# Decoder trunk, one core: cache loads moved to GpSimd's queue, and another order at the end of the first norm

## The chip, the cores and the metric

The kernel runs on one core of a Trainium2 chip. The metric is the device time of one execution in microseconds (us), the median over several runs. A profile is one execution under the hardware profiler. Its engines are PE (TensorE matmul), DVE (VectorE), ACT (ScalarE), POOL (GpSimd) and SP (SyncE, which issues most transfers).

## The reference, cut to what matters

One decoder layer runs on 1024 prompt tokens and on 8 decode samples that share the weights. All arithmetic is float32.

```python
z = x @ w_in                                   # all branches and gates in one projection
# branch C, decode: each sample attends to its own 256 memory tokens, 4 heads of width 256
s = jnp.einsum('bthd,bmhd->bhtm', q, mk).astype(jnp.float32) * (XHEAD_DIM ** -0.5)
p = jax.nn.softmax(s, axis=-1).astype(mv.dtype)
...
return jnp.einsum('bhtm,bmhd->bthd', p, mv).reshape(B, T, XW)
...
h = layer_norm(ALPHA * x + merged @ w_out, ln1_g, ln1_b)        # the first norm
gt, up = jnp.split(h @ w_gate_up, 2, axis=-1)
h = layer_norm(ALPHA * h + (jax.nn.silu(gt) * up) @ w_down, ln2_g, ln2_b)
```

## The kernel before, in words

The 1032 tokens (1024 + 8) lie along the free dimension, the channels along the 128 partitions. Every product is done as three matmuls: each operand is cut into a high part, rounded by ACT (`CAST ..h`, line 79), and a low part, subtracted by DVE (`TENSOR_TENSOR ..l`, line 80), and PE adds high x high, high x low and low x high. A weight's low part is needed for the third matmul of each group only. Most projections use one level of Strassen's scheme: seven products instead of eight, with sums of quarter tiles made by DVE.

**The projection** (about 60 to 690 us) is a list of 30 units of seven products; a product takes PE some 2.9 us, and weights are cut three products ahead. After each product `pump` advances side work by a step: the gated recurrence `lru` and the transposes of the value rows `v_rows` after each one, and `dec_mem`, the decode samples' memory attention, after every second one. `dec_mem` runs once per head (4 heads). Its inner `fetch` loads a 256 KB tile of the key cache (`dck`) or value cache (`dcv`) and, for every second sample, the broadcast row that it is multiplied with (`dckq`, `dcvq`); `dots` then multiplies and sums on DVE (line 840). Each tag has two buffers, so a load waits for the `dots` two samples back. All of these 92 loads are issued by SP, in one queue with the weight loads (`ur`) and the stores. `v_rows` transposes on PE into a PSUM tile of which there is one buffer (`vt`, tag "o"); ACT (line 385) and DVE (line 386) empty it before the next transpose may start.

**The first norm** works by quarters of the tokens. `quarter_norm` of the last quarter (q = 3) ends after the output projection; PE meanwhile runs `plain_gate_up`, the first two feed-forward units f = 0 and 1 done plainly, quarter by quarter: gate product `fg`, ACT's tanh and DVE's line 1170 (`ft`), up product `fu`, DVE's line 1173 (`G`). `ft` releases the PSUM buffer of `fg` (two for even quarters, two for odd ones), `G` that of `fu` (three in all). The norm takes the root on ACT (`n1rs`), the reciprocal on DVE (line 1075), multiplies both halves (`R30`, `R31`; line 1077), applies gain and shift on ACT (line 1082, four steps a half), stores, and cuts into `hh30`/`hl30` and `hh31`/`hl31`. `h_combos` then makes the quarter sums for Strassen (`ht`, `hth`, `htl`, sums written into `R..`). The weights of f = 1 are cut in halves: `wfg10`, `wfg11` for the gate, `wfu10`, `wfu11` for up.

The framework's scheduler sets each engine's order from its own model of time. Each engine then runs its list strictly in that order and waits by semaphores. `tc.issue_after(ins)` keeps what is written inside it behind `ins` in the list of the engine of `ins`.

Of the kernel before, what the change touches and what calls it, by code (L numbers as in the profile page):

```python
# [12 lines left out]
AF = mybir.ActivationFunctionType  # L13
ALU = mybir.AluOpType
# [4 lines left out]
P = 128  # L19
# [22 lines left out]
QN = T // 4  # L42
# [16 lines left out]
V_G1, V_B1, V_G2, V_B2, V_SNK, V_SNKD, V_EPS, V_N = 88, 96, 104, 112, 120, 136, 137, 138  # L59


class Builder:
# [754 lines left out]
    def dec_mem(self, h):  # L817

        nc, io, ph = self.nc, self.io, self.dp
        qr = self.dram.tile([NB, 256], F32, name=f"dcq{h}")  # L820
        self.dec_rows(self.qdc, 2 * h, qr, "c")
        sc = ph.tile([P, 2, NB], F32, tag="dsc", name=f"dcs{h}", bufs=1)
        rows = {}

        def fetch(kind, b, src, row=None):
            if row is not None and b % 2 == 0:
                rows[kind] = ph.tile([P, 512], F32, tag="dq", name=f"dc{kind}q{b}_{h}", bufs=2)
                nc.sync.dma_start(rows[kind].rearrange("p (b d) -> p b d", b=2), row[b:b + 2, :].partition_broadcast(P))
            t = ph.tile([P, 512], F32, tag="dk", name=f"dc{kind}{b}_{h}", bufs=2)
            nc.sync.dma_start(t.rearrange("p (t d) -> p t d", t=2), src)  # L830
            return t

        keys = lambda b: fetch("k", b, io["cmk"][b, :, h * 256:(h + 1) * 256].rearrange("(t p) d -> p t d", p=P), qr)
        vals = lambda b, row: fetch("v", b, io["cmvT"][b, h * 256:(h + 1) * 256, :].rearrange("(f p) k -> p f k", p=P),
                                    row)

        def dots(t, row, b, dst):
            for e in range(2):
                junk = ph.tile([P, 256], F32, tag="dj", name=f"dcj{b}_{h}_{e}", bufs=1)
                nc.vector.scalar_tensor_tensor(junk, t[:, e * 256:(e + 1) * 256], 1.0,  # L840
                                               row[:, (b % 2) * 256:(b % 2 + 1) * 256], op0=ALU.mult, op1=ALU.mult,
                                               accum_out=dst(e))

        nxt = keys(0)
        yield
        for b in range(NB):
            t, row = nxt, rows["k"]
            nxt = keys(b + 1) if b + 1 < NB else vals(0, None)
            dots(t, row, b, lambda e: sc[:, e, b:b + 1])
            yield  # L850
        ps = self.bank("o", f"dct{h}")
        for kt in range(2):
            nc.tensor.transpose(ps[:NB, kt * P:(kt + 1) * P], sc[:, kt, :], self.ident)
        pr = ph.tile([NB, 256], F32, tag="dp", name=f"dcp{h}", bufs=1)
        st = self.sm.tile([P, 8], F32, tag="cst", name=f"dcst{h}", bufs=4)
        nc.vector.tensor_reduce(st[:NB, 0:1], ps[:NB, :256], axis=AX.X, op=ALU.max, negate=True)
        nc.scalar.activation(pr, ps[:NB, :256], AF.Exp, bias=st[:NB, 0:1], scale=1.0, accum_out=st[:NB, 1:2])
        nc.vector.reciprocal(st[:NB, 2:3], st[:NB, 1:2])
        nc.vector.tensor_scalar_mul(pr, pr, st[:NB, 2:3])
        pd = self.dram.tile([NB, 256], F32, name=f"dcpd{h}")  # L860
        nc.sync.dma_start(pd, pr)
        rows["v"] = ph.tile([P, 512], F32, tag="dq", name=f"dcvq_{h}", bufs=2)
        nc.sync.dma_start(rows["v"].rearrange("p (b d) -> p b d", b=2), pd[0:2, :].partition_broadcast(P))
        yield
        for b in range(NB):
            t, row = nxt, rows["v"]
            nxt = vals(b + 1, pd) if b + 1 < NB else None
            dots(t, row, b, lambda e: self.cdec[:, 2 * h + e, b:b + 1])
            yield
# [187 lines left out]
    def quarter_norm(self, q, s1, h):  # L1057

        nc, r, vec = self.nc, self.R, self.vec
        cast = lambda a: a.unsqueeze(1).to_broadcast([P, 4, QN])  # L1060
        yield
        mu = self.col_mean(s1, QN, f"n1mu{q}")
        sq = []
        for kh in range(2):
            nc.vector.tensor_sub(r[q, kh], r[q, kh], cast(mu))
            sq.append(self.tq.tile([P, 4, QN], F32, tag=f"q{q}{kh}", name=f"sq{q}{kh}", bufs=2))
            nc.scalar.activation(sq[kh], r[q, kh], AF.Square)
        nc.vector.tensor_add(sq[0], sq[0], sq[1])
        nc.vector.tensor_add(sq[0][:, 0:2, :], sq[0][:, 0:2, :], sq[0][:, 2:4, :])
        nc.vector.tensor_add(sq[0][:, 0, :], sq[0][:, 0, :], sq[0][:, 1, :])  # L1070
        yield
        var = self.col_mean(sq[0][:, 0, :], QN, f"n1va{q}")
        rs = self.ph.tile([P, QN], F32, tag="rs", name=f"n1rs{q}", bufs=1)
        nc.scalar.activation(rs, var, AF.Sqrt, bias=vec[:, V_EPS:V_EPS + 1])
        nc.vector.reciprocal(rs, rs)
        for kh in range(2):
            nc.vector.tensor_mul(r[q, kh], r[q, kh], cast(rs))
            h[q, kh] = self.quarter_pair(q, kh, "h")
            for k in range(4):
                m = 4 * kh + k  # L1080
                v = r[q, kh][:, k, :]
                nc.scalar.activation(v, v, AF.Identity, bias=vec[:, V_B1 + m:V_B1 + m + 1],
                                     scale=vec[:, V_G1 + m:V_G1 + m + 1])
            nc.sync.dma_start(self.scr["h"][:, 4 * kh:4 * kh + 4, q * QN:(q + 1) * QN], r[q, kh])
            self.split(*h[q, kh], r[q, kh])
        self.norm_end = self.last_lo
# [70 lines left out]
    def plain_gate_up(self, f, h, steps):  # L1157

        nc, io = self.nc, self.io
        wg = self.weights(io["wgu"][f], D, f"wfg{f}")  # L1160
        wu = self.weights(io["wgu"][NF + f], D, f"wfu{f}")
        out = self.zt(f"G{f}")
        for q in range(4):
            x = [tuple(a[:, k % 4, :] for a in h[q, k // 4]) for k in range(KT)]
            pg = self.bank(("s", "t")[q % 2], f"fg{f}_{q}")[:, :QN]
            self.mm3(pg, list(zip(wg, x)))
            self.norm_step()
            t = self.ph.tile([P, QN], F32, tag="gt", name=f"ft{f}_{q}", bufs=3)
            nc.scalar.activation(t, pg, AF.Tanh, scale=0.5)
            nc.vector.scalar_tensor_tensor(t, t, 1.0, pg, op0=ALU.add, op1=ALU.mult)  # L1170
            pu = self.bank("mm", f"fu{f}_{q}")[:, :QN]
            self.mm3(pu, list(zip(wu, x)))
            nc.vector.tensor_mul(out[:, q * QN:(q + 1) * QN], t, pu)
            if f or q:
                with self.tc.issue_after(self.norm_end):
                    next(steps, None)
        nc.sync.dma_start(self.scr["f"][:, f, :], out)
# [281 lines left out]
class FinishDown:  # L1459


    scale = SHARE
# [158 lines left out]
```

## Time and profile before

| | |
|---|---|
| median of 3 runs | 1936.51 us (1936.05 to 1939.27) |
| profiled execution | 1938.83 us, of which the span 1937.1 us |
| granted PE clock | 0.995 of full speed |
| POOL transfers issued | 16 stores of memory keys and values, 16 accumulating stores near the end |
| bytes moved | 303.20 MB, 157 GB/s over the span |

A row of a group of instructions gives line, engine, operation, output<-input, count, then busy time in us and mean ns of one, then the idle time just before them and what ended it. A row of the timeline gives start, duration, engine, line, and in brackets the idle time before it with what it waited for. A row of the waits gives who waited for whom, the total in us, the number of times and the longest.

### The profile page before, as it was taken

To read this page: it belongs to the slowest core of one execution; us is meant where nothing else is said; L and a number is where in the kernel's file an instruction comes from. 1 tells how busy PE (TensorE), PEld (TensorE's weight loads), DVE (VectorE), ACT (ScalarE), POOL (GpSimd) and SP (SyncE) were. 2 spreads that over 40 slices of the span, in tenths; PEclk is the share of its full clock that TensorE was granted. 3 is DMA by queue.
4 is the path that set the end of the run, shared out by engine and by line. 5 is a ranking of instruction groups with operands and counts; after the bars stand their busy time and mean duration, and the time that the engine had idled before them with its cause. 6 is when DMAs were issued, how large, how long until landed. Compare 5 with 4: busy or idle time off the path is not lost.

```text
span 1937.1 us, 37999 instructions
## 1 busy us (share of the span) xinstructions
PE 1901.0 (98%) x14716; PEld 1869.5 (97%) x14716; DVE 1389.0 (72%) x2738; ACT 1001.8 (52%) x2115; POOL 117.0 (6%) x168
## 2 busy tenths in 40 slices
PE   9999999999999999999999999999999999999996
PEld 8999999999999998888899999999999999999996
DVE  7878887877866655378887557775667667858467
ACT  6555565555655644388775234543433434636424
POOL 1000001110000000022110000000000000001001
PEclk9999999999999999999999999999999999999998
DMA  8545555446423376667534351123245345768542
GB/s 308 179 146 173 168 182 167 140 150 210 169 83 137 117 240 222 196 173 208 152 98 152 110 197 58 60 99 99 93 154 195 96 134 182 254 161 233 137 143 88
DMA packets 171637, 303.20 MB, mean 157 GB/s; under 512 B 19568, under 2 KB 86208, under 8 KB 171456
## 3 DMA queue, kind: packets, MB, share of 16 engines
q1 hardware_dynamic: 168384, 290.22, 45.8%
q0 software_dynamic: 3072, 10.55, 2.7%
q8 instruction: 115, 1.88, 0.4%
q14 instruction: 66, 0.54, 0.1%
HBM read 214.79 MB, written 90.09 MB: 157 GB/s over the span
## 4 chain that ended last, share of the span: by engine, by line
PE 84%; ACT 5%; DMA 4%; DVE 4%; issue 1%; SPq 0%; ACTq 0%; DVEq 0%
PE ub L250 5%; PE ub L248 5%; PE ub L249 5%; PE ubfg L248 4%; PE ubfg L249 4%; PE ubfg L250 4%; PE ud L250 3%; PE ud L249 3%; PE ud L248 3%; PE udfg L248 2%; PE udfg L249 2%; PE udfg L250 2%; PE op L120 2%; PE op L122 2%; PE op L121 2%; PE brs L120 2%
## 5 line engine op out<-in xcount | busy, mean ns | idle before, releaser
L605 ACT ACTIVATE bp<-bp,bst 128x257 f32<-128x257 f32 (+1 forms) x128 | 62.8, 493 | 17.7 <-DVE bst L601 17.3
L248 PE MATMUL ub<-th,u_4h 128*128 128x258 f32 x240 | 67.8, 283 | 1.3 <-ACT u2s L274 1.3
L248 PE MATMUL ub<-th,u_0h 128*128 128x258 f32 x240 | 68.0, 284 | 0.7 <-ACT zb L1490 0.6
L250 PE MATMUL ub<-th,u_4l 128*128 128x258 f32 x240 | 68.2, 284 | 0.0
L250 PE MATMUL ub<-th,u_0l 128*128 128x258 f32 x240 | 68.2, 284 | 0.0
L250 PE MATMUL ub<-th,u_2l 128*128 128x258 f32 x240 | 68.2, 284 | 0.0
L250 PE MATMUL uc<-th,u_3l 128*128 128x258 f32 x240 | 68.2, 284 | 0.0
L250 PE MATMUL ud<-th,u_1l 128*128 128x258 f32 x240 | 68.1, 284 | 0.0
L250 PE MATMUL ud<-th,u_5l 128*128 128x258 f32 x240 | 68.1, 284 | 0.0
L250 PE MATMUL ub<-th,u_6l 128*128 128x258 f32 x240 | 68.1, 284 | 0.0
L248 PE MATMUL ub<-th,u_6h 128*128 128x258 f32 x240 | 67.9, 283 | 0.0
L248 PE MATMUL uc<-th,u_3h 128*128 128x258 f32 x240 | 67.9, 283 | 0.0
L248 PE MATMUL ub<-th,u_2h 128*128 128x258 f32 x240 | 67.8, 283 | 0.0
L248 PE MATMUL ud<-th,u_5h 128*128 128x258 f32 x240 | 67.8, 282 | 0.0
L248 PE MATMUL ud<-th,u_1h 128*128 128x258 f32 x240 | 67.7, 282 | 0.0
L249 PE MATMUL ub<-tl,u_6h 128*128 128x258 f32 x240 | 67.7, 282 | 0.0
L249 PE MATMUL ud<-tl,u_5h 128*128 128x258 f32 x240 | 67.7, 282 | 0.0
L249 PE MATMUL uc<-tl,u_3h 128*128 128x258 f32 x240 | 67.6, 282 | 0.0
L249 PE MATMUL ub<-tl,u_4h 128*128 128x258 f32 x240 | 67.6, 282 | 0.0
L249 PE MATMUL ud<-tl,u_1h 128*128 128x258 f32 x240 | 67.6, 282 | 0.0
L249 PE MATMUL ub<-tl,u_0h 128*128 128x258 f32 x240 | 67.6, 282 | 0.0
L249 PE MATMUL ub<-tl,u_2h 128*128 128x258 f32 x240 | 67.6, 282 | 0.0
(954 smaller groups left out, 8228.3 us busy)
## 6 DMA issues: line engine op xcount, KB each, us to landing
ur<-win SPq DMA_DIRECT2D x120, 256.0 KB, 2.9
urfg<-wgu SPq DMA_DIRECT2D x80, 256.0 KB, 2.6
scr_f<-G SPq DMA_DIRECT2D x22, 516.0 KB, 3.2
f<-scr_f SPq DMA_DIRECT2D x16, 516.0 KB, 5.7
fs<-scr_t SPq DMA_DIRECT2D x16, 516.0 KB, 8.3
dck<-cmk SPq DMA_DIRECT2D x32, 256.0 KB, 3.7
dcv<-cmvT SPq DMA_DIRECT2D x32, 256.0 KB, 2.8
st<-scr_q SPq DMA_DIRECT2D x32, 256.0 KB, 5.1
```

Of the source, the lines that this page charges most:

```text
L120: nc.tensor.matmul(ps, sh, mh, start=opens and i == 0, stop=False)
L121: nc.tensor.matmul(ps, sh, ml, start=False, stop=False)
L122: self.last_mm = nc.tensor.matmul(ps, sl, mh, start=False, stop=closes and i == last).ins
L248: mm(sh[:, w], xh, start=opens and k == 0, stop=False)
L249: mm(sh[:, w], xl, start=False, stop=False)
L250: self.last_mm = mm(sl[:, w], xh, start=False, stop=k == 3).ins
L605: nc.scalar.activation(x, x, AF.Exp, bias=st[:, g:g + 1], scale=-1.0, accum_out=st[:, 4 + g:5 + g])
```

## The change

`fetch` issues its loads of cache tiles and of row pairs from GpSimd's queue instead of SP's (64 + 28 transfers). The first row pair of the values (line 863 before) stays on SP. Two more `yield`s let `dec_mem` pause one step longer ahead of its first load and ahead of its first value `dots`. In `quarter_norm`, the third and fourth gain-and-shift step of each half of the last quarter go from ACT to DVE. In `plain_gate_up`, `G` of quarters 0 and 1 is kept behind the norm's last reciprocal, `G` of quarters 2 and 3 behind the last `hl`.

```diff
@@ fetch, in dec_mem
-                nc.sync.dma_start(rows[kind].rearrange("p (b d) -> p b d", b=2), row[b:b + 2, :].partition_broadcast(P))
+                nc.gpsimd.dma_start(rows[kind].rearrange("p (b d) -> p b d", b=2), row[b:b + 2, :].partition_broadcast(P))
             t = ph.tile([P, 512], F32, tag="dk", name=f"dc{kind}{b}_{h}", bufs=2)
-            nc.sync.dma_start(t.rearrange("p (t d) -> p t d", t=2), src)
+            nc.gpsimd.dma_start(t.rearrange("p (t d) -> p t d", t=2), src)
@@ dec_mem
+        yield
         nxt = keys(0)
         yield
...
         nc.sync.dma_start(rows["v"].rearrange("p (b d) -> p b d", b=2), pd[0:2, :].partition_broadcast(P))
+        yield
         yield
@@ quarter_norm
-        nc.vector.reciprocal(rs, rs)
+        self.norm_root = nc.vector.reciprocal(rs, rs).ins
...
-                nc.scalar.activation(v, v, AF.Identity, bias=vec[:, V_B1 + m:V_B1 + m + 1],
-                                     scale=vec[:, V_G1 + m:V_G1 + m + 1])
+                gain, shift = vec[:, V_G1 + m:V_G1 + m + 1], vec[:, V_B1 + m:V_B1 + m + 1]
+                if q == 3 and k > 1:
+                    nc.vector.tensor_scalar(v, v, gain, shift, op0=ALU.mult, op1=ALU.add)
+                else:
+                    nc.scalar.activation(v, v, AF.Identity, bias=shift, scale=gain)
@@ plain_gate_up
-            nc.vector.tensor_mul(out[:, q * QN:(q + 1) * QN], t, pu)
+            with self.tc.issue_after(self.norm_root if q < 2 else self.norm_end):
+                nc.vector.tensor_mul(out[:, q * QN:(q + 1) * QN], t, pu)
```

The lists of the engines move in two places of the program, the projection and the end of the first norm. The lines after the edits are numbered up to six higher, so `ft` is L1175 and `G` L1179 in the new kernel.

**First place: DVE at the end of the norm's last quarter.** In these names the two digits after `R`, `hh`, `hl` are quarter and half, and those after `ft` and `fu` are f and quarter. Before:

```order
L1173 TENSOR_TENSOR G0_16171<-ft0_1_16297,fu0_1_16300 128x258
L1075 RECIPROCAL n1rs3_16274<-n1rs3_16274 128x258
L1077 TENSOR_TENSOR R30_15877<-R30_15877,n1rs3_16274 128x1032
L1077 TENSOR_TENSOR R31_15879<-R31_15879,n1rs3_16274 128x1032
L1170 SCALAR_TENSOR_TENSOR ft0_2_16357<-ft0_2_16357,fg0_2_16332 128x258
L1173 TENSOR_TENSOR G0_16171<-ft0_2_16357,fu0_2_16360 128x258
L80 TENSOR_TENSOR hl30_16279<-R30_15877,hh30_16278 128x1032
```

The same place now:

```order
L1077 RECIPROCAL n1rs3_16274<-n1rs3_16274 128x258
L1179 TENSOR_TENSOR G0_16171<-ft0_1_16297,fu0_1_16300 128x258
L1079 TENSOR_TENSOR R30_15877<-R30_15877,n1rs3_16274 128x1032
L1079 TENSOR_TENSOR R31_15879<-R31_15879,n1rs3_16274 128x1032
L1086 TENSOR_SCALAR R30_15877<-R30_15877,vec_65 128x258 x2
L1086 TENSOR_SCALAR R31_15879<-R31_15879,vec_65 128x258 x2
L1175 SCALAR_TENSOR_TENSOR ft0_2_16357<-ft0_2_16357,fg0_2_16332 128x258
L80 TENSOR_TENSOR hl30_16279<-R30_15877,hh30_16278 128x1032
```

The reciprocal stands ahead of `G` of quarter 1, four gain-and-shift steps are added, and `G` of quarter 2 is gone from ahead of `hl30`.

**Second place: DVE just behind, where `h_combos` and the weights of f = 1 are made, and PE there.** `wfg10_l` is the low part of the first half of f = 1's gate weights. DVE before, from the last `hl` on:

```order
L80 TENSOR_TENSOR hl31_16289<-R31_15879,hh31_16288 128x1032
L1145 TENSOR_TENSOR ht1_0_16326<-R00_15043,R20_15611 128x1032
L80 TENSOR_TENSOR wfg10_l_16459<-wfg1r0__16456,wfg10_h_16458 128x512
L1148 TENSOR_TENSOR R20_15611<-R21_15613,R20_15611 128x1032
L80 TENSOR_TENSOR htl1_0_16329<-ht1_0_16326,hth1_0_16328 128x1032
L1149 TENSOR_TENSOR R00_15043<-R20_15611,R00_15043 128x1032
```

DVE now:

```order
L80 TENSOR_TENSOR hl31_16289<-R31_15879,hh31_16288 128x1032
L1150 TENSOR_TENSOR ht1_0_16326<-R00_15043,R20_15611 128x1032
L1179 TENSOR_TENSOR G0_16171<-ft0_2_16357,fu0_2_16360 128x258
L1153 TENSOR_TENSOR R20_15611<-R21_15613,R20_15611 128x1032
L80 TENSOR_TENSOR htl1_0_16329<-ht1_0_16326,hth1_0_16328 128x1032
L1154 TENSOR_TENSOR R00_15043<-R20_15611,R00_15043 128x1032
L1175 SCALAR_TENSOR_TENSOR ft0_3_16417<-ft0_3_16417,fg0_3_16392 128x258
L80 TENSOR_TENSOR htl4_0_16447<-R20_15611,hth4_0_16446 128x1032
L91 SCALAR_TENSOR_TENSOR htl2_0_16389<-R00_15043,hth2_0_16388 128x1032
L1179 TENSOR_TENSOR G0_16171<-ft0_3_16417,fu0_3_16420 128x258
L1158 TENSOR_TENSOR R00_15043<-R00_15043,R01_15045 128x1032
L80 TENSOR_TENSOR wfg10_l_16459<-wfg1r0__16456,wfg10_h_16458 128x512
```

`wfg10_l` went from second behind the last `hl` to eleventh. PE now, from the last matmul of f = 0 on (before, the last row here followed the first one at once):

```order
L122 MATMUL fu0_3_16420<-hh31_16288,wfu01_l_16168 128x258
L120 MATMUL fu1_0_16509<-hh00_15482,wfu10_h_16470 128x258
L121 MATMUL fu1_0_16509<-hl00_15483,wfu10_h_16470 128x258
L120 MATMUL fu1_1_16569<-hh10_15748,wfu10_h_16470 128x258
L121 MATMUL fu1_1_16569<-hl10_15749,wfu10_h_16470 128x258
L120 MATMUL fg1_3_16664<-hh30_16278,wfg10_h_16458 128x258
L121 MATMUL fg1_3_16664<-hl30_16279,wfg10_h_16458 128x258
L120 MATMUL fu1_2_16629<-hh20_16014,wfu10_h_16470 128x258
L121 MATMUL fu1_2_16629<-hl20_16015,wfu10_h_16470 128x258
L122 MATMUL fg1_0_16481<-hh00_15482,wfg10_l_16459 128x258
```

Eight matmuls that need no low part moved ahead of the first that does. The two on `fg1_3` reuse the PSUM buffer of `fg0_3`, those on `fu1_2` the one of `fu0_3`.

**Third place: DVE in the projection, beside the transposes of the value rows.** `v0` to `v7` are the value rows, `dcj` the output of `dots` (digits: sample, head, half), `u18_..`, `us19_..` the weight parts and sums of units 18 and 19. Before:

```order
L386 TENSOR_TENSOR v2_6237<-vt2_6234,v2_6237 128x4x64
L80 TENSOR_TENSOR u18_4l_6299<-us18_4_6296,u18_4h_6298 128x512
L232 TENSOR_TENSOR us19_2_6511<-us19_1_6475,ur19_00_6288 128x512
L386 TENSOR_TENSOR v3_6278<-vt3_6275,v3_6278 128x4x64
L840 SCALAR_TENSOR_TENSOR dcj5_3_0_6565,dcs3_6032<-dck5_3_6469,dckq4_3_6380 128x256
L840 SCALAR_TENSOR_TENSOR dcj5_3_1_6567,dcs3_6032<-dck5_3_6469,dckq4_3_6380 128x256
L80 TENSOR_TENSOR u18_5l_6342<-us18_5_6339,u18_5h_6341 128x512
L232 TENSOR_TENSOR us19_4_6613<-ur19_00_6288,ur19_10_6292 128x512
L386 TENSOR_TENSOR v4_6335<-vt4_6332,v4_6335 128x4x64
```

The same place now:

```order
L386 TENSOR_TENSOR v2_6201<-vt2_6198,v2_6201 128x4x64
L80 TENSOR_TENSOR u18_4l_6263<-us18_4_6260,u18_4h_6262 128x512
L232 TENSOR_TENSOR us19_2_6465<-us19_1_6429,ur19_00_6252 128x512
L386 TENSOR_TENSOR v3_6242<-vt3_6239,v3_6242 128x4x64
L80 TENSOR_TENSOR u18_5l_6306<-us18_5_6303,u18_5h_6305 128x512
L232 TENSOR_TENSOR us19_4_6567<-ur19_00_6252,ur19_10_6256 128x512
L386 TENSOR_TENSOR v4_6299<-vt4_6296,v4_6299 128x4x64
```

Before, six of the eight key `dots` of head 3 stood between `v0` and `v5`. Now none stands between `v0` and `v7`: the value `dots` of head 2 are all ahead of `v0`, the key `dots` of head 3 come in units 18 and 19 behind `v7`.

## The prediction

> **What bounds the kernel now.** I read the page first, then busy time by stage, then what PE waits for.
>
> ```profile
> span 1937.1 us, 37999 instructions
> PE 1901.0 (98%) x14716; PEld 1869.5 (97%) x14716; DVE 1389.0 (72%) x2738; ACT 1001.8 (52%) x2115; POOL 117.0 (6%) x168
> ```
>
> ```profile
> 60.00:520.00 460.00, 456.17 (x3754) 454.26 (x3753) 375.99 (x813) 262.86 (x503) 35.72 (x41) 1.00 0.50 165
> 1100.00:1300.00 200.00, 198.73 (x1584) 197.83 (x1582) 145.98 (x232) 86.15 (x143) 0.00 (x0) 1.00 0.30 101
> 1400.00:1700.00 300.00, 299.93 (x2494) 299.72 (x2493) 210.22 (x312) 130.17 (x251) 0.00 (x0) 1.00 0.50 168
> ```
>
> The columns are the stretch, its length, then busy us of PE, PEld, DVE, ACT and POOL, granted clock, share of DMA time and GB/s. PE is the bound. Where nothing delays it, a matmul passes every 299.93 / 2494 = 0.120 us, at full clock. The change removes no matmul, so it can only move PE's idle time: 460 - 456.2 = 3.8 us in the projection and 1.3 us around the first norm. PE's waits name it, first for 60 to 520 us, then for 1195 to 1700 us:
>
> ```profile
> PE vt L374 <- DVE v L386: 1.8, 3, 0.9
> PE ub L248 <- ACT u2s L274: 1.3, 1, 1.3
> PE ub L248 <- ACT zb L1490: 0.6, 1, 0.6
> ```
>
> ```profile
> PE fg L120 <- ACT hh L79: 0.8, 1, 0.8
> PE fg L121 <- DVE hl L80: 0.5, 1, 0.5
> ```
>
> **Part 1: the loads on GpSimd's queue, and the two added yields.** The 1.8 us are three waits of PE for a `vt` buffer that DVE had not emptied. DVE's timeline shows why:
>
> ```profile
> 442.77 0.43 DVE L840 SCALAR_TENSOR_TENSOR dcj<-dck,dckq 128x256 f32<-128x256 f32 x1 [1.30 <-DMA dck<-cmk]
> 448.72 0.43 DVE L840 SCALAR_TENSOR_TENSOR dcj<-dck,dckq 128x256 f32<-128x256 f32 x1 [2.57 <-DMA dck<-cmk]
> ```
>
> DVE stood 1.30 and 2.57 us at a `dots` whose tile had not landed, with the value row queued behind it. SP could not issue the load earlier; its queue was in order too:
>
> ```profile
> SPq L830 <- DVE dcj L840: 55.2, 30, 4.6
> ```
>
> In 30 of the 64 loads SP itself stood waiting for the buffer, 55.2 us in all, with whatever came next behind it. In the new order no `dots` stands between `v0` and `v7`, so all 1.8 us go: -1.8 us. The other two waits in the projection are these:
>
> ```profile
> 70.89 0.39 PE L248 MATMUL ub<-th,u_4h 128*128 128x258 f32 x1 [1.31 <-ACT u2s L274]
> 509.38 0.39 PE L248 MATMUL ub<-th,u_0h 128*128 128x258 f32 x1 [0.58 <-ACT zb L1490]
> ```
>
> The one at 509 us follows a late ACT step beside head 3's value `dots`. These move to later units, but ACT's own steps stay; I take -0.4 between -0.6 and 0. At 70 us the first unit runs and no `dots` has; I leave that wait.
>
> What it adds: POOL gets 92 transfers. No POOL load is in this trace; the nearest rows are its stores at the start, beside SP's loads of these tiles, and the recurrence's POOL steps.
>
> ```profile
> L401 POOL DMA_DIRECT2D scr_mk<-mkr x8: 539/542/741, 14.0 to 35.3; - x8
> L757 POOL COPY pconv<-za 128x3 f32<-128x3 f32 x8 | 13.5, 1691 | 131.4 <-DVE za L281 131.4
> L759 POOL COPY scvo<-za 128x8 f32<-128x8 f32 x8 | 6.6, 827 | 0.0
> ```
>
> ```profile
> DMA to landing us min/median/max: 4.5/5.6/5.9
> DMA to landing us min/median/max: 2.7/3.7/4.3
> ```
>
> The first landing row is POOL's stores `mkr`, the second SP's loads `dck`. The `mkr` row gives least, median and greatest ns of an issue: 0.54 us makes 92 x 0.54 = 50 us on an engine busy 36 of 460 us: harmless in itself. A load may land between 1 us sooner and 3 us later after its issue than now; I take some 2 us later, near POOL's own row, though at 30 places it is issued with nothing but its buffer ahead. A `dots` then makes DVE wait about as much as today, which is
>
> ```profile
> DVE dcj L840 <- DMA dcv<-cmvT: 9.2, 10, 3.1
> DVE dcj L840 <- DMA dck<-cmk: 8.5, 7, 2.6
> DVE dcj L840 <- DMA dckq<-dcq: 6.7, 4, 2.8
> ```
>
> 24 us, and little of it reached PE except at `vt`, since weights are cut three products (3 x 24 matmuls x 0.120 = 8.6 us) ahead. The longest new chain is in unit 19: the loads of samples 6 and 7 of head 3 stand on POOL behind `pconv`, which waits for DVE's last `za` of that unit. From there it is 1.69 + 0.83 + 5.6 = 8.1 us to sample 6's tile. Behind that `dots` DVE holds `u20_4l`, which PE needs five products later, at 5 x 2.9 = 14.4 us. So 6 us of cover are left for DVE to catch up: 0 us, bounds 0 and +4 (if a wait of 2 us shows through at this place and at its twin in unit 22). Part 1: -2.2 us, from -2.4 to +2.
>
> The Trainium skill speaks against this part: "SBUF — State Buffer", section "Who interferes with whom", says that a VectorE instruction in a two-port mode locks GpSimd out, so that a transfer issued there lacks its descriptors. Here the eight `mkr` stores took 0.54 to 0.74 us to issue beside DVE's cutting of operands, so the trace shows no such hold so far; DVE's steps in the projection are nearly all of the two-input kind of which the page says that they meet only GpSimd's reads. If it held here, part 1 would give less; its price is with the rivals.
>
> **Part 2: the end of the first norm.** What stands there now, ACT and DVE in order of time, and PE's two late starts:
>
> ```profile
> 1240.95 0.48 ACT L1074 ACTIVATE n1rs<-n1va3p,vec 128x258 f32<-128x258 f32 x1
> 1242.30 0.42 DVE L1173 TENSOR_TENSOR G<-ft,fu 128x258 f32<-128x258 f32 x1 [2.17 <-PE fu L122]
> 1242.64 1.76 DVE L1075 RECIPROCAL n1rs<-n1rs 128x258 f32<-128x258 f32 x1
> 1244.43 2.38 DVE L1077 TENSOR_TENSOR R<-R,n1rs 128x1032 f32<-128x1032 f32 x2
> 1245.19 0.39 ACT L1169 ACTIVATE ft<-fg 128x258 f32<-128x258 f32 x1 [2.46 <-PE fg L122]
> 1245.70 2.58 ACT L1082 ACTIVATE R<-R,vec 128x258 f32<-128x258 f32 x5
> 1248.19 1.04 ACT L79 CAST hh<-R 128x1032 fp32r<-128x1032 f32 x1
> 1249.26 1.23 DVE L80 TENSOR_TENSOR hl<-R,hh 128x1032 fp32r<-128x1032 f32 x1 [0.77 <-ACT hh L79]
> 1251.84 1.23 DVE L80 TENSOR_TENSOR hl<-R,hh 128x1032 fp32r<-128x1032 f32 x1 [1.35 <-ACT hh L79]
> 1252.99 1.23 DVE L1145 TENSOR_TENSOR ht<-R,R 128x1032 f32<-128x1032 f32 x1
> 1254.13 0.68 DVE L80 TENSOR_TENSOR wfg_l<-wfg1r__16456,wfg_h 128x512 fp32r<-128x512 f32 x1
> 1254.73 1.23 DVE L1148 TENSOR_TENSOR R<-R,R 128x1032 f32<-128x1032 f32 x1
> 1258.17 0.41 DVE L1170 SCALAR_TENSOR_TENSOR ft<-ft,fg 128x258 f32<-128x258 f32 x1
> 1258.50 1.23 DVE L80 TENSOR_TENSOR htl<-R,hth 128x1032 fp32r<-128x1032 f32 x1
> ```
>
> ```profile
> 1249.28 0.39 PE L120 MATMUL fg<-hh,wfg_h 128*128 128x258 f32 x1 [0.76 <-ACT hh L79]
> 1250.54 0.38 PE L121 MATMUL fg<-hl,wfg_h 128*128 128x258 f32 x1 [0.52 <-DVE hl L80]
> ```
>
> *The norm gets shorter.* The root is ready at 1240.95 + 0.48 = 1241.43, yet the reciprocal waits behind `G`. Now it starts at about 1241.5 and ends at 1243.3; `G` takes 0.34 (start to start, 1258.17 to 1258.50), the two multiplications end at 1246.05. DVE's four new steps are priced by
>
> ```profile
> L514 DVE TENSOR_SCALAR cp<-cp,cst 128x256 f32<-128x256 f32 x32 | 9.8, 350 | 0.5
> ```
>
> 4 x 0.35 = 1.4 us, until 1247.45, the first two by 1246.75. ACT, after its `ft` at 1245.58, does three steps of 2.58 / 5 = 0.52 to 1247.15, then `hh30` to 1248.2 instead of 1249.23; one more step and `hh31` to 1249.75. So `hl30` ends at 1249.5 instead of 1250.49, and `hl31` starts at 1249.75 instead of 1251.84. PE is at `hh30` at 1249.28 - 0.76 = 1248.52: no wait. Four matmuls later it waits for `hl30` to 1249.55: 0.55 us. So far PE is 1.0 us ahead.
>
> *Then DVE is late for f = 1.* PE has 46 matmuls left of f = 0 (to 1249.55 + 46 x 0.120 = 1255.05) and four of `fu1_0` and `fu1_1` (1255.55). The next ones need DVE. By the rows above, DVE's steps follow each other at 1.15 us (128x1032), 0.34 (128x258) and 0.60 (128x512). From `ht` at 1250.9: `G` of quarter 2 1252.05, `R` 1252.4, `htl` 1253.55, `R` 1254.7, `ft` of quarter 3 1255.85 to 1256.25, `htl` 1256.2, `htl` 1257.5 (0.15 late for ACT's `hth`), `G` of quarter 3 1258.65 to 1259.05, `R` 1259.0, `wfg10_l` 1260.1 to 1260.8. PE waits for that `ft` from 1255.55 to 1256.25 (0.7), does two matmuls, waits for that `G` from 1256.5 to 1259.05 (2.55), does two, and waits for `wfg10_l` from 1259.3 to 1260.8 (1.5). Sum of waits: 0.55 + 0.7 + 2.55 + 1.5 = 5.3 against 1.3 now. Counted another way: 178 matmuls are left at 1260.8, so the plain units end at 1282.2; now 232 are left at 1250.54, end 1278.4: +3.8. I take +3.9. Later stretches run at 299.93 of 300 us and give nothing back. The bounds: -0.8, if `wfg10_l` is never waited for, and +4.6, if each of DVE's eleven steps starts 0.06 later.
>
> What holds this up is that a matmul that needs only high parts is in front, and then DVE's list is in the way; before, `wfg10_l` came in time (1254.81), and PE had 40 matmuls that needed only it.
>
> **Sum.** -1.8 - 0.4 + 3.9 = +1.7 us. The profiled execution took 1938.83 us, 1.73 of them outside its span, and lies 2.3 above the median; a like one would take 1940.5. On the median: 1936.51 + 1.7 = **1938.2 us**. About 0.2%, 3.9 us, is what a measurement can tell from no change (the three runs spread by 3.2 us).
>
> **Rivals.**
>
> *Order costs nothing at the norm.* DVE runs ahead of my replay, or PE's wait is covered, and the norm gives 0.8 us. For it: its end is 2.1 us earlier for `hl31`. Against: eleven DVE steps, 9.2 us, stand in front of `wfg10_l`, and PE has 50 matmuls, 6 us. Time: 1936.5 - 0.8 - 2.2 = 1933.5. Chance 0.12.
>
> *GpSimd's chain shows through (slower).* Place: samples 6 and 7 of head 3 in unit 19, sample 7's values in unit 22. It decides when a tile lands more than 14.4 - 0.6 us behind the last `za`, or when DVE's backlog outlasts the 6 us of cover. For it: DVE is busy 82% here. Against: today's 24 us of such waits reached PE at `vt` alone. Price +4: 1938.2 + 4 = 1942.2. Chance 0.20.
>
> *The queue is no matter.* PE keeps the projection's waits, because DVE is late at `vt` for its own work. For it: DVE's share. Against: the 1.30 and 2.57 us stood at a load. Time 1936.5 + 3.9 = 1940.4. Chance 0.10. The Trainium skill's "DMA: Bandwidth & Descriptors", section "Issuing engines are not separate DMA queues", has it that another issuing engine saves only the time to initiate a transfer; by that, this rival holds. The trace disagrees so far, in that SP's waits of 55.2 us were for buffers and not for issuing.
>
> *Issues on POOL are held by DVE.* The 21 loads on which DVE waits today (10, 7 and 4 times, above) come later, each by as much as the longest of the rows allows, 1.69 - 0.54 = 1.15 us if an issue takes as long as `pconv`: 24 us more of DVE's waiting. Today's 24 us put 1.8 on PE: +1.8, 1940.0. Against: `mkr` at 0.54. Chance 0.03. It is the rule of the page on SBUF above.
>
> **Numbers.** The forecast has 0.55, with 1936.8 to 1939.8 as its own range. The range 1934.0 to 1943.0 takes in the slower rival and half of the first. Slower by over 0.2% (above 1940.4): nearly all of the GpSimd rival, half of the third, a little of my own: 0.27. Faster (below 1932.6): a third of the first rival and little else, since PE's idle time in both places is only 5.1 us: 0.05. Within: 0.68.
>
> **What would show it.** Right: no wait of PE at `vt`, and between 1249 and 1262 three waits on `fg1_3`, `fu1_2` and `fg1_0` of about 0.7, 2.5 and 1.5 us, released by DVE's `ft`, `G` and `wfg_l`; `hh30` about 1 us earlier. Wrong: new waits of PE in 60 to 520 us for low parts `u_..l` or recurrence operands with DVE standing at `dcj`; or a stretch from 1249 to 1262 without waits.

## The result and the profile after

The changed kernel takes 1944.39 us (median of 6 runs, 1942.08 to 1945.32) against 1935.77 us (6 runs, 1932.01 to 1939.27): a ratio of 1.0041, with a 95% interval from 1.0031 to 1.0052. It is slower by 6 to 10 us, where +1.7 us was forecast.

Three instructions of PE mark the stages in every kernel here: the first and last matmul on `u_0l` (start and end of the projection's list), the first on `n1va3p` (the last quarter's norm), and the first on `ubfg` (the first Strassen unit behind the plain ones). Each row ends in the first and the last start. The kernel before:

```profile
L250 PE MATMUL ub<-th,u_0l x240: 279/284/368, 58.1 to 678.0; 128*128 128x258 f32 x120
L953 PE MATMUL n1va3p<-n1va3h,ones x1: 385/385/385, 1239.7 to 1239.7; 128*128 128x258 f32 x1
L248 PE MATMUL ubfg<-hh,ufg_0h x160: 277/282/289, 1278.7 to 1665.2; 128*128 128x258 f32 x160
```

The changed kernel:

```profile
L250 PE MATMUL ub<-th,u_0l x240: 279/284/293, 56.7 to 679.9; 128*128 128x258 f32 x120
L955 PE MATMUL n1va3p<-n1va3h,ones x1: 386/386/386, 1240.1 to 1240.1; 128*128 128x258 f32 x1
L248 PE MATMUL ubfg<-hh,ufg_0h x160: 277/282/289, 1284.5 to 1670.9; 128*128 128x258 f32 x160
```

The projection grew from 619.9 to 623.2 us (+3.3; forecast -2.2), the stretch from there to the last norm shrank from 561.7 to 560.2 (-1.5; the kernels of experiments 2 and 4, which change nothing ahead of the last norm, took 562.1 and 560.0 us there, so this is not shown to come from the change), and the norm with the plain units grew from 39.0 to 44.4 us (+5.4; forecast +3.9). That is +7.2 us, inside the interval, and +8.7 us in the two places that the change touches. (The first mark itself, which the change doesn't touch, lies anywhere from 56.5 to 58.5 us in the fourteen profiles of this study. Here it is 1.4 us earlier, and the stretch behind the last mark 0.6 us shorter, so the two profiled executions as a whole differ by 5.3 us only.)

PE's waits in the changed kernel, from 60 to 520 us and then from 1195 to 1700 us:

```profile
PE vt L374 <- DVE v L386: 2.1, 1, 2.1
PE ub L248 <- DVE zb L278: 1.3, 2, 1.0
PE ub L248 <- ACT u2s L274: 1.3, 1, 1.3
PE ub L248 <- ACT p1s L274: 1.1, 1, 1.1
PE ub L248 <- ACT zb L1498: 0.4, 2, 0.2
```

```profile
PE fu L120 <- DVE G L1179: 2.1, 1, 2.1
PE fg L122 <- DVE wfg_l L80: 0.9, 1, 0.9
PE fg L120 <- DVE ft L1175: 0.5, 1, 0.5
PE fg L121 <- DVE hl L80: 0.3, 1, 0.3
```

In the projection the three waits at `vt` have become one, but a longer one, and new waits stand on `zb` and `p1s`. In the norm the three forecast waits are there, in order and nearly in size. With the short one for `hl` they sum to 3.9 us against 1.3 before. So 2.6 of the 5.4 us are waits; most of the rest, 2.1 us by experiment 3, has another cause, which the granted clock shows.

**The projection.** DVE's list in the changed kernel, where the value `dots` of head 2 now run:

```profile
412.58 0.43 DVE L840 SCALAR_TENSOR_TENSOR dcj<-dcv,dcvq 128x256 f32<-128x256 f32 x1 [2.13 <-DMA dcv<-cmvT]
414.37 0.42 DVE L840 SCALAR_TENSOR_TENSOR dcj<-dcv,dcvq 128x256 f32<-128x256 f32 x1 [0.88 <-DMA dcv<-cmvT]
416.80 0.42 DVE L278 SCALAR_TENSOR_TENSOR zb<-ub,p5s 128x258 f32<-128x258 f32 x1
433.55 0.08 DVE L840 DVE_READ_ACCUMULATOR dcj<-dcv,dcvq 128x1 f32 x1
438.02 0.42 DVE L840 SCALAR_TENSOR_TENSOR dcj<-dcv,dcvq 128x256 f32<-128x256 f32 x1 [2.16 <-DMA dcv<-cmvT]
441.00 0.42 DVE L386 TENSOR_TENSOR v<-vt,v 128x256 fp32r<-128x256 f32 x1
```

What PE waited for there:

```profile
417.27 0.39 PE L248 MATMUL ub<-th,u_6h 128*128 128x258 f32 x1 [1.05 <-DVE zb L278]
441.47 0.33 PE L374 MATMUL vt<-ident,za 128*128 128x128 f32 x1 [2.09 <-DVE v L386]
```

DVE stands 3.0 us at two tiles that have not landed (and 1.57 us at a row pair just before them, at 406.98); `zb`, which empties a PSUM buffer that PE needs at once, comes late behind them. At 438.02 DVE stands 2.16 us at the last sample's tile, and the first value row comes late behind that. The load of that tile, on POOL:

```profile
434.04 0.72 POOL L830 DMA_DIRECT2D dcv<-cmvT  x1 [4.08 <-DVE dcj L840]
```

Its buffer was free when the `dots` two samples back ended, at 433.55 + 0.08 = 433.63 us. POOL began the issue 0.41 us later and took 0.72 us for it. On SP before, one such pair of rows:

```profile
438.83 0.08 DVE L840 DVE_READ_ACCUMULATOR dcj<-dck,dckq 128x1 f32 x1
438.94 0.38 SPq L830 DMA_DIRECT2D dck<-cmk  x1
```

There the issue followed the freed buffer by 0.03 us and took 0.38 us.

**The norm.** PE in the changed kernel:

```profile
1255.76 0.28 PE L121 MATMUL fu<-hl,wfu_h 128*128 128x258 f32 x1
1256.58 0.39 PE L120 MATMUL fg<-hh,wfg_h 128*128 128x258 f32 x1 [0.54 <-DVE ft L1175]
1259.20 0.58 PE L120 MATMUL fu<-hh,wfu_h 128*128 128x258 f32 x1 [2.12 <-DVE G L1179]
1260.95 0.58 PE L122 MATMUL fg<-hh,wfg_l 128*128 128x258 f32 x1 [0.94 <-DVE wfg_l L80]
1261.33 0.42 PE L120 MATMUL fg<-hh,wfg_h 128*128 128x258 f32 x1
```

A matmul behind the wait shows 0.42 us where one ahead shows 0.28. Busy time of PE in five stretches of 3.41 us (the stretch, its length, PE's busy us and matmuls, the granted clock, share of DMA time, GB/s):

```profile
1252.04:1255.45 3.41, 3.41 (x31) 1.00 0.00 0
1255.45:1258.86 3.41, 1.10 (x8) 1.00 0.01 2
1258.86:1262.27 3.41, 2.12 (x8) 0.50 0.48 170
1262.27:1265.69 3.42, 3.42 (x18) 0.50 0.75 235
1265.69:1269.10 3.41, 3.41 (x30) 1.00 0.16 62
```

After a stretch in which PE was busy 1.10 of 3.41 us, the granted clock was half for two such stretches; the second of them passed 18 matmuls where a full one passes 30. In the trace of before the granted clock is full throughout these stages.

### The profile page after: what moved, and what is told of

Its sections match the earlier page's. It is cut to its first block, busy times and chain, and to the rows that moved or that the text cites. A ratio compares the mean times of both kernels' runs of the same rounds, so it can differ in the third digit from the quotient of the medians.

```text
span 1942.3 us, 38063 instructions
## 1 busy us (share of the span) xinstructions
PE 1904.7 (98%) x14716; PEld 1873.3 (96%) x14716; DVE 1389.3 (72%) x2742; ACT 997.2 (51%) x2111; POOL 170.7 (9%) x260
## 4 chain that ended last, share of the span: by engine, by line
PE 85%; ACT 5%; DVE 5%; DMA 4%; issue 2%; POOL 0%; SPq 0%; ACTq 0%; DVEq 0%; POOLq 0%
PE ub L250 5%; PE ub L248 5%; PE ub L249 5%; PE ubfg L248 4%; PE ubfg L249 4%; PE ubfg L250 4%; PE ud L250 2%; PE ud L249 2%; PE ud L248 2%; PE udfg L248 2%; PE udfg L249 2%; PE udfg L250 2%; PE op L120 2%; PE op L122 2%; PE op L121 2%
## 5 line engine op out<-in xcount | busy, mean ns | idle before, releaser
L1479 POOL DMA_DIRECT2D scr_h<-zaf x8 | 7.0, 878 | 797.8 <-DVE zaf L281 797.8
```

The lines of the kernel that those rows point to most:

```text
L1479: self.b.nc.gpsimd.dma_start(self.b.scr["h"][:, m, :], z, accum_op=ALU.add)
```

## The experiments

All times are compared with the kernel before on the same chip; each interval is 95%.

**1. The loads and the pauses alone** (label p1): `fetch` on `nc.gpsimd`, both `yield`s, the norm as before.

> The loads on GpSimd and the two pauses alone, the norm as before. Theory 1 (the trace of the changed kernel read stage by stage): PE loses 3.4 us in the projection, behind value products of the decode attention that stand ahead of the first value transpose, and the attention stage gives 1.5 of it back: +1.9 us. Theory 2 (as the prediction had it): PE's waits at the transposes go, -2.2 us. Theory 3 (the loss of the changed kernel is nearly all here): +6 us or more.

Measured: 1.0028 (1.0017 to 1.0039), 1942.74 against 1937.29 us, the projection 57.9 to 683.4 us in its marks, +5.6. Theory 2, the prediction's own step, is out. The interval, +3.3 to +7.6 us, leaves out theory 1's +1.9 as well and reaches theory 3's +6: more of the loss is here than the changed kernel's trace showed. The waits of PE are those of the changed kernel, 2.0 us at the first `vt` among them; but here the clock fell too:

```profile
439.30:442.71 3.41, 1.38 (x12) 1.00 0.39 141
442.71:446.12 3.41, 3.41 (x17) 0.50 0.58 208
```

The same wait cost more in this profile than in the changed kernel's, where the clock stayed full at this place: 17 matmuls instead of 30 are some 1.6 us (13 x 0.120, an estimate).

**2. The norm alone** (label p2): the edits of `quarter_norm` and `plain_gate_up`, the loads on SP without pauses.

> The edits of the norm alone, the loads as before. Theory 1: PE waits for hl, ft, G and wfg_l, 3.9 us in sum, and the granted clock falls to half for 3.4 or 6.8 us behind the wait for G: +5.3 us. Theory 2 (the fall of the clock belongs to the whole changed kernel's timing, not to this wait): the same waits at a full clock, +3.9 us as predicted. Theory 3 (the projection carries the loss): between -0.8 and +1 us.

Measured: 1.0028 (1.0019 to 1.0038), 1943.33 us; 43.9 us from `n1va3p` to `ubfg`, +4.9. The clock was half for one stretch of 3.41 us, from 1260.74 us on. It is theory 1 by the trace; the time's interval, +3.7 to +7.4 us, has room for theory 2's +3.9 too.

**3. The norm alone, with PE kept busy in the wait** (label p2_fill).

```diff
             pg = self.bank(("s", "t")[q % 2], f"fg{f}_{q}")[:, :QN]
+            if f == 1 and q == 3:
+                for _ in range(22):
+                    nc.tensor.matmul(pg, wg[0][0], x[0][0], start=True, stop=True)
```

> The edits of the norm alone, with 22 idle matmuls on PE between the wait for ft and the wait for G (22 x 0.120 = 2.6 us; they write the gate's PSUM bank, which the real products then start anew). Theory 1 (the idle stretch of 3 us makes the granted clock fall): no half clock between 1255 and 1270 us; the wait for G nearly gone, the one for wfg_l still there, and as the matmuls behind it then run at 0.120 instead of 0.215 us for some 4.7 us, this kernel is 2 us faster than the one without the idle matmuls, +3.3 us against before. Theory 2 (the clock is no matter, the waits are): within 0.3 us of the kernel without them, or later by what they take.

Measured: 42.3 us from mark to mark, +3.3 instead of +4.9, and no fall of the clock. In the trace, the same five stretches as above:

```profile
1252.04:1255.45 3.41, 3.41 (x30) 1.00 0.00 0
1255.45:1258.86 3.41, 2.88 (x24) 1.00 0.02 5
1258.86:1262.27 3.41, 2.44 (x20) 1.00 0.45 170
1262.27:1265.69 3.42, 3.42 (x31) 1.00 0.76 237
1265.69:1269.10 3.41, 3.41 (x31) 1.00 0.14 55
```

The idle matmuls do nothing useful and PE still ends this stage 1.6 us earlier. In both kernels the wait for `wfg_l` ends 20.9 us behind the mark `n1va3p`, so all of the 1.6 us arises behind it, where the clock differs. In time it is 1.0024 (1.0015 to 1.0033), 1941.81 us: in the expected direction, but the intervals of 2 and 3 overlap, so the gain is shown by the trace and not by the times.

**4. The norm without the tie of `G` to the last `hl`** (label n_tsroot).

```diff
-            with self.tc.issue_after(self.norm_root if q < 2 else self.norm_end):
+            with self.tc.issue_after(self.norm_root) if q < 2 else nullcontext():
                 nc.vector.tensor_mul(out[:, q * QN:(q + 1) * QN], t, pu)
```

> The edits of the norm without the tie of G of quarters 2 and 3 to the last hl: the reciprocal still stands ahead of G of quarter 1 and four gain-and-shift steps are on DVE, but G of quarter 2 is ahead of hl30 again and wfg10_l second behind hl31. Theory 1 (the tie moves wfg10_l, and that is what PE waits for): no wait of PE for G or wfg_l, the waits for hh and hl shrink from 1.3 to 0.3 to 0.9 us: -0.4 to -1.0 us against before, not to be told from no change. Theory 2 (the four steps on DVE delay h_combos and the weights by 1.4 us): a wait for wfg_l of 1 us or more, +1 to +2 us.

Measured: 1.0000 (0.9989 to 1.0012); 37.9 us from mark to mark, -1.1. The one wait of PE left from 1195 to 1700 us, and DVE behind the last `hl`:

```profile
PE fg L121 <- DVE hl L80: 0.7, 1, 0.7
```

```profile
1248.19 1.23 DVE L1148 TENSOR_TENSOR ht<-R,R 128x1032 f32<-128x1032 f32 x1
1249.34 0.69 DVE L80 TENSOR_TENSOR wfg_l<-wfg1r__16456,wfg_h 128x512 fp32r<-128x512 f32 x1
1255.99 0.41 DVE L1177 TENSOR_TENSOR G<-ft,fu 128x258 f32<-128x258 f32 x1
```

Theory 1: with the tie gone, the scheduler puts `wfg10_l` second again, and no wait is left on `G` or `wfg_l`. In the trace the reciprocal's new place and the four steps on DVE give 1.1 us (the interval of the time has room for that and for nothing); the tie alone turns that into a loss.

**5. and 6. GpSimd's queue without the pauses, and the pauses without GpSimd's queue** (labels pool, yld).

> The 92 loads on GpSimd without the two pauses; the norm as before. Theory 1 (the pauses do the harm: they slide the value products of head 2 from units 15 to units 16 and 17, where the last of them stands right ahead of the first value transpose's row): within 1 us of before. Theory 2 (GpSimd's queue does it: an issue takes 0.72 us instead of 0.38 and the tile of values lands after 3.5 instead of 2.8 us): +3 to +5 us, with longer waits of PE at the transposes than today's 1.8 us, since the key products of head 3 still stand between them.

> The two pauses alone, the loads on SP; the norm as before. Theory 1 (the pauses): +3 to +5 us like both together, with PE waits at zb of unit 17 and at the first transpose of about 1 and 2 us. Theory 2 (the queue): 0 to -2 us, no wait of PE over 0.5 us at the transposes; the last value tile of head 2 then lands about 1.1 us earlier than on GpSimd, which takes the wait at the first transpose from 2.1 to 1.0 us.

Measured: the queue alone 1.0085 (1.0065 to 1.0104), 1953.17 us (4 runs; the profiled one, at 1946.53, was the fastest of them); the pauses alone 0.9994 (0.9984 to 1.0004), 1936.45 us. The marks of the queue alone, then of the pauses alone:

```profile
L250 PE MATMUL ub<-th,u_0l x240: 279/284/364, 57.5 to 690.1; 128*128 128x258 f32 x120
```

```profile
L250 PE MATMUL ub<-th,u_0l x240: 276/284/288, 56.8 to 674.9; 128*128 128x258 f32 x120
```

In these traces the queue costs 12.7 us in the projection (one window of half clock, at 446 us, is in it) and the pauses gain 1.8. Theory 1 falls and theory 2 holds, with three times its price. With the pauses PE's waits at `vt` go from 1.8 to 0.7 us, since no key `dots` of head 3 stand between the value rows any more. The time of the pauses alone cannot be told from no change. So the pauses are what the first part needed; on GpSimd they only soften the harm.

The queue's edit changes more than the landing. The kernels with the pauses on SP and on GpSimd do not run the same lists, since the scheduler orders DVE anew when the queue changes. With the pauses on SP, these are the end of the `dots` that frees the buffer for the last value tile of head 2, the load of that tile and the `dots` that reads it:

```profile
430.12 0.08 DVE L840 DVE_READ_ACCUMULATOR dcj<-dcv,dcvq 128x1 f32 x1
430.31 0.38 SPq L830 DMA_DIRECT2D dcv<-cmvT  x1
433.89 0.42 DVE L840 SCALAR_TENSOR_TENSOR dcj<-dcv,dcvq 128x256 f32<-128x256 f32 x1
```

Here 3.7 us lie between the freed buffer (430.20) and the `dots`, which does not wait. In the changed kernel DVE is ready for this `dots` at 438.02 - 2.16 = 435.86, only 2.2 us behind the freed buffer, because one sum `us`, one `za` and the cut `u_0l`, which on SP stand between the two, no longer do. With SP's 0.03 + 2.8 us that list would have waited some 0.6 us, with GpSimd's landing (4.4 us from the freed buffer here) SP's list some 0.7 us; both together wait 2.16. These are estimates: no run changes the queue and keeps the lists, so how much of the queue's cost is the later landing and how much the new order is not shown.

**7. Three buffers for the cache tiles** (label p1_b3: queue and pauses; label pool_b3: queue alone). The two other tiles with the tag `dk`, in the later window attention, get three buffers as well.

```diff
-            t = ph.tile([P, 512], F32, tag="dk", name=f"dc{kind}{b}_{h}", bufs=2)
+            t = ph.tile([P, 512], F32, tag="dk", name=f"dc{kind}{b}_{h}", bufs=3)
```

> Loads on GpSimd and both pauses as in the changed kernel, the norm as before, and three buffers instead of two for the tiles of the key and value cache, so that a load waits for the products three samples back. Theory 1 (DVE stands at products whose load could not start before a buffer came free: 3.9 us from the free buffer to the landing, over two samples): DVE's waits for dck and dcv fall from 19.6 us to under 8, PE's waits in the projection from 6.2 to under 4 us, and the time is 2 us or more below that with two buffers. Theory 2 (DVE is late for its own work there, loads or not): the same waits of PE, within 1 us of two buffers.

> The loads on GpSimd without pauses, with three buffers for the cache tiles. Theory 1 (GpSimd makes each load land about 1 us later behind a freed buffer, 4.0 instead of 2.8 to 3.3 us, and with two buffers that delay stands in DVE's list every second sample): a third buffer gives a load one sample more, DVE's waits for dck and dcv fall from 28.0 us to under 12 and PE's loss in the projection from 12.7 to under 6 us. Theory 2 (GpSimd's issue holds DVE or its queue is blocked by other steps of GpSimd): the third buffer is no help, still +10 us or more.

Measured with the pauses: 1.0012 (1.0002 to 1.0022), 1940.36 us, DVE's waits for `dck` and `dcv` 8.5 us, PE's waits in the projection 4.1 us; the projection +1.8 us instead of +5.6. As theory 1 had it, but for a little; the gain is shown by the trace, while the intervals of the times still touch. Without the pauses: 1.0063 (1.0050 to 1.0077), 1949.29 us, and the projection still +12.9 us, with the clock at half twice there. DVE's waits for `dck` and `dcv` fell to 20.2 us, not under 12. So theory 1's simple chain (one buffer more, one delay less) does not carry that kernel, and theory 2's figure came (+12.2 us in time). Its second reason is not what the loads show: 56 of the 61 that reuse a buffer began within 1 us of its being free, the latest 3.1 us behind. The loads took longer on the way, 3.9 us for `dcv` and 4.2 for `dck` at the median, against 3.4 and 3.7 with two buffers. Why a third buffer helps with the pauses and hardly without them stays open.

**8. The loads on ACT's queue, with the pauses** (label act_yld): `nc.scalar.dma_start` in `fetch`.

> Both pauses, and the 92 loads issued by ACT instead of SP or GpSimd; the norm as before. Theory 1 (the longer way from a freed buffer to a landed tile is GpSimd's own): an issue takes about as long as on SP, 0.38 us, and follows the freed buffer within 0.1 us instead of 0.41, so tiles land after about 2.8 to 3.3 us. Theory 2 (any queue apart from SP's, where loads no longer stand in one list with the weights, is as slow): 0.7 us an issue and 4.0 us to the landing. For the time this kernel is no clean test, since ACT's own steps now stand behind loads that wait for DVE: with theory 1 anything from the -0.8 us of the pauses on SP to +10 us.

Measured: 1.0049 (1.0030 to 1.0068), slow for the reason named, ACT's list. Issue times in ns (least, median, greatest) and the way from issue to landing of the value tiles, all three with the same pauses: on SP (label yld), on ACT, and on POOL in the changed kernel:

```profile
L830 SPq DMA_DIRECT2D dcv<-cmvT x32: 368/379/1757, 112.0 to 548.3; - x32
DMA to landing us min/median/max: 2.6/2.8/3.9
```

```profile
L830 ACTq DMA_DIRECT2D dcv<-cmvT x32: 374/374/752, 114.2 to 556.4; - x32
DMA to landing us min/median/max: 2.6/2.8/4.6
```

```profile
L830 POOL DMA_DIRECT2D dcv<-cmvT x32: 704/722/762, 113.8 to 555.3; - x32
DMA to landing us min/median/max: 3.0/3.5/4.4
```

Theory 1: the longer way is GpSimd's own. From the freed buffer to the landing it is 0.03 + 2.8 us on SP and 0.41 + 3.5 on GpSimd, some 1.1 us more for a value tile. For the key tiles the medians from issue to landing are 2.8, 3.1 and 3.6 us in the same three kernels; without the pauses they are 3.7 us on SP (before) and 3.7 on GpSimd (label pool), so this part of the difference depends on the kernel. GpSimd's other steps did not hold the loads up: of the 62 loads that reuse a buffer, all began within 1 us of its being free in the changed kernel and in that of the queue alone, 60 and 61 of them within 0.5 us.

**9. The harmless parts together** (label yld_tsroot: pauses on SP and the norm of experiment 4; label yld_b3_tsroot: three buffers as well; label b3_tsroot: three buffers, without pauses).

> The two parts that did no harm, together: both pauses with the loads on SP, and the edits of the norm without the tie of G of quarters 2 and 3 (reciprocal ahead of G of quarter 1, four gain-and-shift steps on DVE). If they add up by their traces: PE gains 1.7 us in the projection and 1.2 in the norm, -2.9 us against before, about -0.15%, faster by an interval that may just exclude no change. If the attention stage takes back what the projection gains (its waits end on transfers that are not earlier): -1.2 us.

> As the kernel with both pauses, loads on SP and the norm without the tie, and a third buffer for the cache tiles. If DVE's remaining waits for dck and dcv (16.1 us with the pauses) still cost PE something: the two waits left in the projection, 0.31 and 0.66 us, go too, -1 us against the same kernel with two buffers. If not: within 0.5 us of it.

> Loads on SP without pauses as before, three buffers for the cache tiles, and the edits of the norm without the tie of G of quarters 2 and 3. If the loads' waits for buffers are behind today's 1.8 us at the transposes, -1 us there, and -1.2 us in the norm as its own run showed: -2 us against before. If the key products themselves hold DVE there: -1.2 us, not to be told from no change.

Measured: 0.9984 (0.9975 to 0.9993), 1934.54 us; 0.9982 (0.9973 to 0.9991), 1934.16 us; 0.9991 (0.9982 to 1.0000), 1935.49 us; before 1937.39, 1937.39 and 1937.26. The first two beat both kernels, by about 3 us against before and 0.57% against the changed one, if the two ratios to before are divided. Projection -1.6 and norm -1.0 us in the trace of the first make -2.6, inside its interval of -4.8 to -1.4 us. Once the pauses are there, the third buffer is worth nothing that can be measured. The third kernel's time, -1.7 us, cannot tell its two expectations apart (interval -3.5 to 0). Its trace does: PE's waits at `vt` are 1.55 and 1.08 us, more than before, so without the pauses a third buffer on SP gives nothing there.

## Why the prediction was wrong

**The step that failed: the price of GpSimd's queue, taken as 0 us.** The prediction held that a load comes some 2 us later there, that DVE then waits about as much as today, and that little of it reaches PE because weights are cut three products ahead. The first two claims held within their bounds: a value tile comes 1.1 us later, and DVE's waits at `dots` for tiles and row pairs are 27.4 us in the changed kernel (12.7 for value tiles, 12.0 for key tiles, 2.7 for row pairs) against 24.7 before. The third did not. Cutting ahead covers `u_..l` alone. Behind a standing `dots` there are also `zb` and the first value row, which empty PSUM buffers that PE wants within a product or less, and they have no such cover. With the pauses gaining 1.8 us on SP, the queue costs 5.1 us in the changed kernel's trace and 7.4 in that of experiment 1, which has a window of half clock there. That the price belongs to the queue is shown (experiments 5 and 6); its division between later landings and DVE's new order stays open.

**The gain at `vt` was right in its cause, for the kernel with the loads on SP, and too large:** in experiment 6 the three waits are gone but a new one of 0.7 us stands at the first value row, so 1.1 of the 1.8 us came. The wait of 0.58 us at 509 us went too. The projection's -1.8 us in its marks stands against the -2.2 that was forecast for both; that it equals the figure for `vt` is chance. The prediction saw that no `dots` stands between `v0` and `v7`. It did not ask what stands right ahead of `v0`: the last value `dots` of head 2, whose tile came 2.16 us late on GpSimd.

**The norm was right in its mechanism, and one term was missing.** The waits for `hl`, `ft`, `G` and `wfg_l` were forecast at 0.55, 0.7, 2.55 and 1.5 us and were 0.33, 0.54, 2.12 and 0.94. Without the fall of the clock the stage costs +3.3 us (experiment 3) against the +3.9 that were forecast. The fall adds 1.6 to 2.1 us, by the traces of experiment 2 and of the changed kernel; the prediction took matmuls at full clock behind every wait. The Trainium skill's page "TensorE: Matmul & The Clock Gate", section "HAM oscillation — how this bites in real kernels", warns of an idle gap that crosses a window of about 3.4 us: it puts PE at half its clock for what follows. The trace agrees in the step, since the clock changed for stretches of 3.41 us, and differs in the length: the longest single gap of PE there was 2.12 us, and a window that was a third busy was enough.

**The rivals.** "GpSimd's chain shows through" was the right one in engine, sign and nearly in price (+4 and 1942.2 us in all), wrong in its place and its chain: units 17 and 18, not 19 and 22, and no `pconv` stood in front of the loads that counted; they began some 0.4 us behind their freed buffers. "The queue is no matter" is refuted by experiments 5 and 6. Its page, "DMA: Bandwidth & Descriptors" of the Trainium skill, has in another section, "Latency and other measured facts", about 0.6 us to the first byte from SP or ACT and about 1 us from GpSimd; the runs agree in sign and show more, 0.7 us from issue to landing of a value tile and 1.1 us from buffer to landing. "POOL issues are held by DVE" is not what happened: all 32 issues of value tiles took 0.70 to 0.76 us, whatever DVE did beside them.

**The range** left out the measured time by 1.4 us. Its upper end was the GpSimd rival alone; the clock was in none of the cases.

## What to carry to other kernels

Price a transfer that moves to another queue from freed buffer to landing, and then ask of the consumer's engine which step stands behind the waiting one and how much cover that step has: one that empties a PSUM buffer has far less than one that cuts a weight ahead of time. When an order is pinned with an edge, or a transfer moved to another queue, look at what the scheduler moves in exchange; here a tie on one small multiplication pushed the cut that PE needed from second to eleventh place. A wait of PE may cost its length and then half a clock behind it, as those of 2.0 and 2.1 us did here. The windows suggest that waits close together count together (0.54 and 2.12 us lie in or reach into the one with 1.10 us busy); no run tests that.

## What had not been expected of the hardware

The granted clock fell to half after a window of 3.41 us in which PE was busy only in part: 1.10 of 3.41 us in the changed kernel, 1.38 in experiment 1, 0.78 in experiment 2. Nor need the wait be long. In six of the fourteen profiles the attention stage lost one window of half clock at about 760 us, behind a wait of 1.15 us in the changed kernel and of 1.72 us in experiment 2. In others it did not, with a like wait at the same place: 1.26 us before, 1.38 us in experiment 4. So whether a given wait costs the clock differs from profile to profile; what decides it is not shown.
